# Second feed-forward: relu and square of the block chunk two pieces later, and its transposes apart from the ordinary chunk's

## The chip, the core and the metric

One core of one Trainium2 chip runs the whole program. The metric is the device time of one execution in microseconds (us), the median of three runs; one further execution was profiled, and all rows below come from it. TensorE (PE in the rows, PEld for its weight loads) multiplies, VectorE (DVE) and ScalarE (ACT) work elementwise and read PE's results out of the PSUM banks, SyncE (SP) issues the loads of weights.

## The reference

Two transformer blocks on 256 tokens of 2048 features. Only the end of the second one is touched, its feed-forward part:

```python
h2 = rms_norm(x, g_ff[l])
x = x + jnp.square(jax.nn.relu(h2 @ w_ff1[l])) @ w_ff2[l]      # w_ff1: 2048 x 8192, w_ff2: 8192 x 2048
```

All data are float32. The kernel splits each operand into a high part (rounded to PE's format) and a low part (the rest), and adds three products for each product of the reference: high by high, high by low, low by high.

## The kernel before

**Pieces.** A weight matrix is streamed in pieces of 512 KB. For each piece SP loads it into a raw buffer (R, or G for a block piece), ACT rounds it to its high part in W (L230), DVE subtracts to get the low part (L232), and PE multiplies. All engines work their instructions off in the order in which the program was written. That order is written out by a list of jobs: before a piece is multiplied, the splits (L230, L232) of the pieces up to three further on are written, as far as their slots in W have been given up by earlier pieces.

**The second feed-forward** has four groups (`gi`). A group makes 2048 of the 8192 columns of `h2 @ w_ff1` and at once multiplies them into the output. It has two *braids* and then four *down chunks*.

- A braid makes 1024 columns. It weaves an *ordinary chunk* of 8 pieces (called a0 to a7 here; L262 to L264, 12 matmuls of 512 columns each, PSUM banks 4 and 5) with a *block chunk* of 8 pieces (b0 to b7; L315 to L317, 21 matmuls of 256 columns each, Strassen's scheme with seven products for eight, banks 0 to 3). The order is a0 a1 b0 a2 b1 a3 b2 a4 b3 a5 b4 a6 b5 a7, the ordinary chunk's end, b6 b7, the block chunk's end. For a block piece DVE also makes sums of weights ahead of its split (L207 to L209).
- The ordinary chunk's end is relu and square by ACT, from PSUM into `abuf` (in G). The block chunk's end, `fin`, has one copy by ACT (L328), four additions by DVE that put the seven products together into G and `tmp` (L329 to L332), and then relu and square by ACT in place: four instructions (L1191 and L1192, twice).
- PE then needs the 1024 columns with tokens along the free axis: 16 transposes for each chunk pair, 8 of `abuf` and 8 of the block chunk's `half` (L387). Four of them fill one of the two PSUM banks 6 and 7; out of each bank ACT writes the high part into B (L374) and DVE the low part (L375). These 16 transposes with their four L374 and four L375 are one job, `pending`: the first braid's stands in the second braid, behind a2 (fourth piece) and ahead of b1; the second braid's stands in the first down chunk, behind its fourth piece.
- A down chunk has 8 pieces (called p0 to p7) of `w_ff2`, ordinary ones, multiplied with the transposed columns in B.

**The first feed-forward** has braids of the same order; there the block chunk's end is done by DVE, and only one chunk's 8 transposes are `pending`.

Of the kernel before, what the change touches and what calls it, by code (L numbers as in the profile page):

```python
# [19 lines left out]
KT = D // P  # L20
# [5 lines left out]
QW = 256  # L26
PLAIN, MIX, STR = 0, 1, 2
# [44 lines left out]
def body(tc, d, out):  # L72
# [4 lines left out]
    with tc.manual_schedule(), \  # L77
# [7 lines left out]
        G = res.tile([P, 8192], F32, name="G")  # L85
# [5 lines left out]
        tmp = res.tile([P, 512], F32, name="tmp")  # L91
# [4 lines left out]
        def rview(t, off, *dims):  # L96
            n = int(np.prod(dims))
            v = t[:, off : off + n]
            if len(dims) == 2:
                return v.rearrange("p (a b) -> p a b", a=dims[0])  # L100
            if len(dims) == 3:
                return v.rearrange("p (a b c) -> p a b c", a=dims[0], b=dims[1])
            if len(dims) == 4:
                return v.rearrange("p (a b c e) -> p a b c e", a=dims[0], b=dims[1], c=dims[2])
            return v
# [26 lines left out]
        def bank_at(b):  # L132
            return PS[:, b * 512 : (b + 1) * 512]
# [7 lines left out]
        jobs = []  # L141
        before_dma, before_split = {}, {}

        def run(fn):
            jobs.append(("run", fn))

        def stage(m):
            run(lambda: mode.__setitem__(0, m))
# [103 lines left out]
        def piece(src, fn, lo=True, post=None, kind=PLAIN):  # L252
            return ("pc", src, fn, lo, post, kind)
# [7 lines left out]
        def mm3(o, x, w, first, last):  # L261
            pe.matmul(o, x[0], w[0], start=first, stop=False)  # L262
            pe.matmul(o, x[0], w[1], start=False, stop=False)  # L263
            pe.matmul(o, x[1], w[0], start=False, stop=last)  # L264

        def chunk(pair, w, kts, c0, n, evict, row0=0, inject=None, kind=PLAIN, fixed=None):

            items, banks = [], list(fixed or ())

            def mk(j):  # L270
                def fn(h, l):
                    if j == 0 and not fixed:
                        banks.extend([FREE.pop(0) for _ in range(NT)])
                    for q in range(2):
                        kt = 2 * j + q
                        for tok in range(NT):
                            mm3(bank_at(banks[tok])[:, :n], pair(kt, tok), (h[:, q, :], l[:, q, :]), kt == 0, kt == kts - 1)
                return fn

            for j in range(kts // 2):  # L280
                if inject and j in inject:
                    items.append(("run", inject[j]))
                items.append(piece(wsrc(w, row0 + 2 * j, c0, n), mk(j), kind=kind))

            def fin():
                for tok in range(NT):
                    evict(tok, bank_at(banks[tok])[:, :n])
                if not fixed:
                    FREE.extend(banks)

            items.append(("run", fin))
            return items

        def strassen(pair, forms, w, kts, c0, evict):

            items = []

            prod = [(("x", 0, 0), 0, 2, 1), (("x", 1, 0), 1, 0, 0), (("s", 3), 2, 3, 0), (("x", 1, 1), 6, 2, 0),  # L300
                    (("s", 0), 3, 1, 1), (("s", 1), 5, 0, 1), (("s", 2), 4, 1, 0)]

            def mk(j):
                def fn(h, l):
                    opened = set()
                    for x, wi, bank, half in prod:
                        o = PS[:, bank * 512 + half * QW : bank * 512 + (half + 1) * QW]
                        if x[0] == "x":
                            xh, xl = pair(2 * j + x[1], x[2])
                        else:  # L310
                            xh, xl = forms[:, 0, j, x[1], :], forms[:, 1, j, x[1], :]
                        first = j == 0 and bank not in opened
                        opened.add(bank)
                        last = j == kts // 2 - 1
                        pe.matmul(o, xh, h[:, wi, :], start=first, stop=False, skip_group_check=True)  # L315
                        pe.matmul(o, xl, h[:, wi, :], start=False, stop=False, skip_group_check=True)  # L316
                        pe.matmul(o, xh, l[:, wi, :], start=False, stop=last, skip_group_check=True)  # L317
                return fn

            for j in range(kts // 2):  # L320
                items.append(piece(wsrc(w, 2 * j, c0, 512), mk(j), kind=STR))

            def fin():
                q = PS[:, 0:2048].rearrange("p (a b) -> p a b", a=8)
                u = rview(G, 1024, 4, QW)
                v = tmp.rearrange("p (a b) -> p a b", a=2)
                bc = [P, 2, QW]
                act.copy(v[:, 0, :], q[:, 5, :])  # L328
                dve.tensor_tensor(u[:, 0:2, :], v[:, 0:1, :].to_broadcast(bc), q[:, 0:2, :], op=ALU.add)  # L329
                dve.tensor_tensor(u[:, 2:4, :], u[:, 1:2, :].to_broadcast(bc), q[:, 2:4, :], op=ALU.add)  # L330
                dve.tensor_tensor(v[:, ::-1, :], u[:, 2:3, :].to_broadcast(bc), q[:, 3:5, :], op=ALU.add)
                dve.tensor_tensor(u[:, 3, :], u[:, 3, :], q[:, 6, :], op=ALU.add)  # L332
                evict(0, u[:, 0:4:3, :])
                evict(1, v)

            items.append(("run", fin))
            return items

        def braid(a, b, inject=None):

            pa, pb = [x for x in a if x[0] == "pc"], [x for x in b if x[0] == "pc"]
            order = [pa[0], pa[1]]
            for i in range(6):
                order += [pb[i], pa[i + 2]]
            order += [a[-1], pb[6], pb[7], b[-1]]
            for at in sorted(inject or {}, reverse=True):
                order.insert(at, ("run", inject[at]))
            return order
# [182 lines left out]
        def blocks(nat):  # L531
            return lambda tok, i: nat[:, tok, i * P : (i + 1) * P]
# [259 lines left out]
        for p in range(9):  # L792
            a, b, c = plan[p]
# [54 lines left out]
        pending = wide(oT_late, "w_attn_o", ev_mix, t_mix, None, kts=8, row0=8)  # L848
# [33 lines left out]
        h2T = pairat(A, 0, KT)  # L882
        h2F = rview(C, 0, 2, KT // 2, 4, P)
        pending = wide(mixT, "w_out", ev_res(tmp, inv2), t_x(h2T, "ffn", h2F), pending, last=MIX)


        abuf = rview(G, 0, NT, 512)
# [9 lines left out]
        def t_a(aT, nat, j):  # L897
            return lambda: transposed(nat, aT, list(range(4 * j, 4 * j + 4)))
# [11 lines left out]
        for gi, (c0, nch) in enumerate(groups):  # L910
            aT = pairat(B, 0, 16)
            for j in range(nch):
                c = c0 + j
# [3 lines left out]
                pending = t_a(aT, blocks(abuf), j)  # L917
            lastg = gi == len(groups) - 1
            for oc in range(4):
                inj = {}  # L920
                if pending is not None:
                    inj[nch * 2 - 4 if oc == 0 else 1] = pending
                    pending = None
                ev = ev_res(tmp, inv3)(oc) if lastg else ev_acc(oc)
                jobs.extend(chunk(aT, "w_ffn_down", 4 * nch, oc * 512, 512, ev, row0=4 * c0, inject=inj,
                                  kind=MIX, fixed=DOWN[oc]))
                if lastg:
                    pending = t_x(hT, "mix")(oc)
# [250 lines left out]
        pending = None  # L1179
        for c in range(4):  # L1180
# [3 lines left out]
            pending = t_mer(c)  # L1184

        inv4 = stat(2)
        pending = wide(merT, "w_out_2", ev_res(tmp, inv4), t_x(h2T, "ff", h2F), pending, last=MIX)


        def relu2(o, tok, v):  # L1190
            act.activation(o, v, AF.Relu, scale=inv4[:, tok : tok + 1])  # L1191
            act.activation(o, o, AF.Square)  # L1192
# [3 lines left out]
            v = rview(G, 1024, 4, QW)[:, 0:4:3, :] if tok == 0 else tmp.rearrange("p (a b) -> p a b", a=2)  # L1196
            return v[:, i // 2, (i % 2) * P : (i % 2 + 1) * P]

        def two(f, g):
            return lambda: (f(), g())  # L1200

        def ev_out(c):
            def f(tok, ps):
                xs = xnat[:, tok, c * 512 : (c + 1) * 512]
# [2 lines left out]
            return f  # L1207

        stage(MIX)
        for gi in range(4):  # L1210
            aT = pairat(B, 0, 16)
            for j in range(0, 4, 2):
                c = 4 * gi + j
                jobs.extend(braid(chunk(h2T, "w_ff1_2", KT, c * 512, 512,
                                        lambda tok, ps: relu2(abuf[:, tok, :], tok, ps), kind=MIX, fixed=(4, 5)),
                                  strassen(h2T, h2F, "w_ff1_2", KT, (c + 1) * 512, lambda tok, v: relu2(v, tok, v)),
                                  {4: pending} if pending is not None else None))
                pending = two(t_a(aT, blocks(abuf), j), t_a(aT, half, j + 1))
            for oc in range(4):
                inj = {}  # L1220
                if pending is not None:
                    inj[4] = pending
                    pending = None
                ev = ev_out(oc) if gi == 3 else ev_acc(oc)
                jobs.extend(chunk(aT, "w_ff2_2", 16, oc * 512, 512, ev, row0=16 * gi, inject=inj,
                                  kind=MIX, fixed=DOWN[oc]))

        drive()

# [80 lines left out]
```

## Time and profile before

| | us |
|---|---|
| median of 3 runs | 2766.05 (2765.75 to 2766.68) |
| the profiled execution, its own time | 2765.54 |
| its span, first to last instruction | 2763.8 |
| PE busy in the span | 2722.0 |
| DVE busy | 1854.9 |
| ACT busy | 1404.2 |

The span is what the trace covers; 1.74 us of the execution's own time lie outside it. Busy times overlap between engines. The second feed-forward runs from about 2018 us to the end of the span.

### The profile page before, as it was taken

The numbers are of one execution on the slowest core, as the hardware profiler recorded it, in microseconds if no ns is written. First come the engines' busy times: TensorE is split into PE (matmuls) and PEld (weight loads), VectorE is DVE, ScalarE is ACT, GpSimd is POOL, SyncE is SP. The second block draws the span as 40 slices with busy tenths as digits, with TensorE's granted clock in tenths as the row PEclk, the third lists the DMA queues.
The fourth block names the chain that finished last, engine by engine and source line by source line (L and its number), as shares of the span: only waits on it lengthen the run. The fifth ranks groups of instructions, "written<-read, shape, count | busy, mean of one in ns | idle before, by whom it ended". The sixth has DMA issues, their size and how long they took to land. (4 is left out here: it accounts for less than half of the span.)

```text
span 2763.8 us, 35989 instructions
## 1 busy us (share of the span) xinstructions
PE 2722.0 (98%) x13996; PEld 2285.7 (83%) x13996; DVE 1854.9 (67%) x2233; ACT 1404.2 (51%) x1749; POOL 72.8 (3%) x153
## 2 busy tenths in 40 slices
PE   9999999999999999999999999999989999999999
PEld 8988888888888888888888888888778878877877
DVE  6554677767995799489655565555686685775774
ACT  6544666545554455355555554443554454453553
POOL 1000111000000000000010100000000000000000
PEclk9999999999999999999999999999999999999999
DMA  7666444554555655555464555555554645645545
GB/s 256 210 209 199 160 138 142 179 177 173 206 191 176 213 183 191 185 204 198 156 212 164 199 177 171 191 187 183 174 177 152 202 173 166 210 142 188 201 153 167
DMA packets 143179, 506.66 MB, mean 183 GB/s; under 512 B 16160, under 2 KB 18592, under 8 KB 142496
## 3 DMA queue, kind: packets, MB, share of 16 engines
q1 hardware_dynamic: 142864, 504.31, 54.2%
q8 instruction: 109, 1.79, 0.3%
q14 instruction: 62, 0.51, 0.1%
q10 hardware_dynamic: 144, 0.05, 0.0%
HBM read 502.21 MB, written 2.10 MB: 182 GB/s over the span
## 5 line engine op out<-in xcount | busy, mean ns | idle before, releaser
L232 DVE TENSOR_TENSOR W<-R,W 128x1024 fp32r<-128x1024 f32 (+2 forms) x795 | 943.2, 1208 | 527.6 <-ACT W L230 525.0
L230 ACT CAST W<-R 128x1024 fp32r<-128x1024 f32 (+2 forms) x798 | 810.0, 1035 | 533.2 <-PE PS L264 439.6
L262 PE MATMUL PS<-W,A 128*128 128x512 f32 (+2 forms) x1728 | 678.6, 393 | 5.6 <-ACT W L230 5.4
L263 PE MATMUL PS<-W,A 128*128 128x512 f32 (+2 forms) x1728 | 678.8, 393 | 5.2 <-DVE W L232 5.2
L264 PE MATMUL PS<-W,A 128*128 128x512 f32 (+2 forms) x1728 | 676.4, 391 | 0.0
L262 PE MATMUL PS<-W,B 128*128 128x512 f32 (+1 forms) x1248 | 491.7, 394 | 0.0
L263 PE MATMUL PS<-W,B 128*128 128x512 f32 (+1 forms) x1248 | 489.5, 392 | 0.9 <-DVE W L232 0.9
L264 PE MATMUL PS<-W,B 128*128 128x512 f32 (+1 forms) x1248 | 489.3, 392 | 0.0
L230 ACT CAST W<-G 128x1792 fp32r<-128x1792 f32 x152 | 257.3, 1693 | 316.3 <-PE PS L316 155.3
L263 PEld LDWEIGHTS PS<-W,A 128*128 128x128 f32 x1728 | 324.7, 188 | 75.5 <-DVE W L232 9.2
L262 PEld LDWEIGHTS PS<-W,A 128*128 128x128 f32 x1728 | 324.5, 188 | 74.1 <-ACT W L230 6.3
L264 PEld LDWEIGHTS PS<-W,A 128*128 128x128 f32 x1728 | 324.3, 188 | 73.6
L232 DVE TENSOR_TENSOR W<-G,W 128x1792 fp32r<-128x1792 f32 x152 | 307.1, 2020 | 53.4 <-ACT W L230 53.4
L263 PEld LDWEIGHTS PS<-W,B 128*128 128x128 f32 x1248 | 234.1, 188 | 55.1 <-DVE W L232 2.1
L264 PEld LDWEIGHTS PS<-W,B 128*128 128x128 f32 x1248 | 233.9, 187 | 54.1
L262 PEld LDWEIGHTS PS<-W,B 128*128 128x128 f32 x1248 | 234.0, 188 | 53.9
L315 PE MATMUL PS<-W,C 128*128 128x256 f32 x608 | 170.2, 280 | 0.0
L317 PE MATMUL PS<-W,C 128*128 128x256 f32 x608 | 169.8, 279 | 0.0
L316 PE MATMUL PS<-W,C 128*128 128x256 f32 x608 | 169.6, 279 | 0.0
L315 PE MATMUL PS<-W,A 128*128 128x256 f32 x456 | 130.6, 286 | 0.0
L317 PE MATMUL PS<-W,A 128*128 128x256 f32 x456 | 128.4, 282 | 0.8 <-DVE W L232 0.8
L316 PE MATMUL PS<-W,A 128*128 128x256 f32 x456 | 128.4, 282 | 0.0
(231 smaller groups left out, 2496.5 us busy)
## 6 DMA issues: line engine op xcount, KB each, us to landing
R<-in_w_in_dram SPq DMA_DIRECT2D x224, 512.0 KB, 4.6
R<-in_w_ff_dram SPq DMA_DIRECT2D x192, 512.0 KB, 3.6
R<-in_w_ffn_gate_dram SPq DMA_DIRECT2D x88, 512.0 KB, 4.4
G<-in_w_ffn_up_dram SPq DMA_DIRECT2D x88, 512.0 KB, 3.5
R<-in_w_ffn_down_dram SPq DMA_DIRECT2D x88, 512.0 KB, 3.5
R<-in_w_out_dram SPq DMA_DIRECT2D x64, 512.0 KB, 4.4
G<-in_w_ff_dram SPq DMA_DIRECT2D x64, 512.0 KB, 3.5
R<-in_w_attn_o_dram SPq DMA_DIRECT2D x32, 512.0 KB, 4.4
```

The costliest lines, as they stand in the source:

```text
L230: act.copy(hv, v)
L232: dve.tensor_tensor(lv, v, hv.bitcast(F32), op=ALU.subtract)
L262: pe.matmul(o, x[0], w[0], start=first, stop=False)
L263: pe.matmul(o, x[0], w[1], start=False, stop=False)
L264: pe.matmul(o, x[1], w[0], start=False, stop=last)
L315: pe.matmul(o, xh, h[:, wi, :], start=first, stop=False, skip_group_check=True)
L316: pe.matmul(o, xl, h[:, wi, :], start=False, stop=False, skip_group_check=True)
L317: pe.matmul(o, xh, l[:, wi, :], start=False, stop=last, skip_group_check=True)
```

## The change

The block chunk's relu and square (`ends`) no longer stand at the end of `fin` in the second feed-forward; they become a job of their own. The pending job is cut into three. In the next braid: the 8 transposes of `abuf` behind a0 (T1), `ends` behind a1, the 8 transposes of `half` behind b2 (T2). In the first down chunk: `ends` behind p0, T1 behind p1, T2 behind p3. No instruction is added or dropped, and no load changes its place.

```diff
-        def strassen(pair, forms, w, kts, c0, evict):
+        def strassen(pair, forms, w, kts, c0, evict, later=False):
...
                 dve.tensor_tensor(u[:, 3, :], u[:, 3, :], q[:, 6, :], op=ALU.add)
-                evict(0, u[:, 0:4:3, :])
-                evict(1, v)
+                if not later:
+                    ends()
+
+            def ends():
+                evict(0, rview(G, 1024, 4, QW)[:, 0:4:3, :])
+                evict(1, tmp.rearrange("p (a b) -> p a b", a=2))
 
             items.append(("run", fin))
-            return items
+            return (items, ends) if later else items
...
         stage(MIX)
+        pending = {4: pending}
...
-                jobs.extend(braid(chunk(h2T, "w_ff1_2", KT, c * 512, 512,
-                                        lambda tok, ps: relu2(abuf[:, tok, :], tok, ps), kind=MIX, fixed=(4, 5)),
-                                  strassen(h2T, h2F, "w_ff1_2", KT, (c + 1) * 512, lambda tok, v: relu2(v, tok, v)),
-                                  {4: pending} if pending is not None else None))
-                pending = two(t_a(aT, blocks(abuf), j), t_a(aT, half, j + 1))
+                plain = chunk(h2T, "w_ff1_2", KT, c * 512, 512, lambda tok, ps: relu2(abuf[:, tok, :], tok, ps),
+                              kind=MIX, fixed=(4, 5))
+                block, ends = strassen(h2T, h2F, "w_ff1_2", KT, (c + 1) * 512, lambda tok, v: relu2(v, tok, v), later=True)
+                jobs.extend(braid(plain, block, pending))
+                pending = {1: t_a(aT, blocks(abuf), j), 2: ends, 7: t_a(aT, half, j + 1)}
             for oc in range(4):
-                inj = {}
-                if pending is not None:
-                    inj[4] = pending
+                inj = None
+                if oc == 0:
+                    inj = {1: pending[2], 2: pending[1], 4: pending[7]}
                     pending = None
```

Numbers ahead of a job say in front of which entry of the list it is put. The order on PE, ACT and DVE changes from this; on SP and POOL it stays. From line 334 on, the changed kernel's lines are numbered some four higher: L1195 and L1196 there are L1191 and L1192 here, L378 and L379 are L374 and L375.

ACT where the first braid of a group passes into the second, before. L328 is `fin`'s copy; the casts after the four activations are those of a2, b1, a3, b2:

```order
L328 COPY tmp<-PS 128x256
L1191 ACTIVATE G<-G,st 128x2x256
L1192 ACTIVATE G<-G 128x2x256
L1191 ACTIVATE tmp<-tmp,st 128x512
L1192 ACTIVATE tmp<-tmp 128x512
L230 CAST W<-R 128x1024
L230 CAST W<-G 128x1792
L230 CAST W<-R 128x1024
L230 CAST W<-G 128x1792
L374 CAST B<-PS 128x512 x4
```

The same place on ACT after the change:

```order
L328 COPY tmp<-PS 128x256
L230 CAST W<-R 128x1024
L378 CAST B<-PS 128x512 x2
L230 CAST W<-G 128x1792
L1195 ACTIVATE G<-G,st 128x2x256
L1196 ACTIVATE G<-G 128x2x256
L1195 ACTIVATE tmp<-tmp,st 128x512
L1196 ACTIVATE tmp<-tmp 128x512
L230 CAST W<-R 128x1024
L230 CAST W<-G 128x1792
L230 CAST W<-R 128x1024
L230 CAST W<-G 128x1792
```

The cast of a2, two of the four casts of transposed columns and the cast of b1 now stand ahead of the four activations; the other two L378 follow one cast further down, behind that of a5.

DVE at the same place, before: `fin`'s four additions, the low part of a2, then the sums of b2 and the low part of b1 (the L375 follow ten rows further down):

```order
L329 TENSOR_TENSOR G<-tmp,PS 128x512
L330 TENSOR_TENSOR G<-G,PS 128x512
L331 TENSOR_TENSOR tmp<-G,PS 128x2x256
L332 TENSOR_TENSOR G<-G,PS 128x256
L232 TENSOR_TENSOR W<-R,W 128x1024
L207 TENSOR_TENSOR G<-G 128x512
L208 TENSOR_TENSOR G<-G 128x256
L209 TENSOR_TENSOR G<-G 128x256
L232 TENSOR_TENSOR W<-G,W 128x1792
```

DVE at the same place after the change:

```order
L332 TENSOR_TENSOR G<-G,PS 128x256
L232 TENSOR_TENSOR W<-R,W 128x1024
L379 TENSOR_TENSOR B<-PS,B 128x512 x2
L207 TENSOR_TENSOR G<-G 128x512
L208 TENSOR_TENSOR G<-G 128x256
L209 TENSOR_TENSOR G<-G 128x256
L232 TENSOR_TENSOR W<-G,W 128x1792
```

Two of the four subtractions of transposed columns came forward, between the low part of a2 and that of b1; the other two stand behind the low part of a5.

ACT where the second braid passes into the first down chunk, after the change. The casts are those of p3, then p4 and p5, then p6 and on:

```order
L328 COPY tmp<-PS 128x256
L1195 ACTIVATE G<-G,st 128x2x256
L1196 ACTIVATE G<-G 128x2x256
L1195 ACTIVATE tmp<-tmp,st 128x512
L1196 ACTIVATE tmp<-tmp 128x512
L230 CAST W<-R 128x1024
L378 CAST B<-PS 128x512 x2
L230 CAST W<-R 128x1024 x2
L378 CAST B<-PS 128x512 x2
```

Here the activations keep their place; before, the casts of p3, p4 and p5 stood together, and all four L374 behind them.

## Rows read from the trace of the kernel before

**Rows 1.** The page: its first line, and PE in part 1.

```profile
span 2763.8 us, 35989 instructions
...
PE 2722.0 (98%) x13996; PEld 2285.7 (83%) x13996; DVE 1854.9 (67%) x2233; ACT 1404.2 (51%) x1749; POOL 72.8 (3%) x153
```

**Rows 2.** Waits of PE, 2025 to 2764: total us, times, longest.

```profile
PE PS L387 <- DVE B L375: 23.7, 8, 5.0
PE PS L262 <- ACT W L230: 4.7, 4, 1.2
PE PS L263 <- DVE W L232: 3.8, 5, 0.8
```

**Rows 3.** Timeline of PE, first group, second braid: start, us, [idle before, releaser].

```profile
2049.59 0.40 PE L262 MATMUL PS<-W,A 128*128 128x512 f32 x1
...
2055.28 0.36 PE L315 MATMUL PS<-W,A 128*128 128x256 f32 x1
...
2057.69 0.28 PE L317 MATMUL PS<-W,C 128*128 128x256 f32 x1
2059.15 0.51 PE L262 MATMUL PS<-W,A 128*128 128x512 f32 x1 [1.18 <-ACT W L230]
2060.41 0.50 PE L263 MATMUL PS<-W,A 128*128 128x512 f32 x1 [0.76 <-DVE W L232]
2060.75 0.39 PE L264 MATMUL PS<-W,A 128*128 128x512 f32 x1
...
2063.07 1.03 PE L387 MATMUL PS<-cst,G 128*128 128x128 f32 x8
2069.06 0.41 PE L387 MATMUL PS<-cst,G 128*128 128x128 f32 x1 [4.96 <-DVE B L375]
...
2070.62 0.56 PE L315 MATMUL PS<-W,A 128*128 128x256 f32 x1
...
2072.66 0.28 PE L315 MATMUL PS<-W,A 128*128 128x256 f32 x1
```

**Rows 4.** Timeline of ACT there.

```profile
2055.50 0.72 ACT L1191 ACTIVATE G<-G,st 128x512 f32<-128x512 f32 x1 [5.55 <-DVE G L332]
...
2058.07 1.03 ACT L230 CAST W<-R 128x1024 fp32r<-128x1024 f32 x1
...
2063.71 1.07 ACT L374 CAST B<-PS 128x512 fp32r<-128x512 f32 x2
```

**Rows 5.** Timeline of DVE there.

```profile
2052.94 0.68 DVE L329 TENSOR_TENSOR G<-tmp,PS 128x512 f32<-128x512 f32 x1
...
2055.05 0.41 DVE L332 TENSOR_TENSOR G<-G,PS 128x256 f32<-128x256 f32 x1
2059.13 1.23 DVE L232 TENSOR_TENSOR W<-R,W 128x1024 fp32r<-128x1024 f32 x1 [3.67 <-ACT W L230]
...
2061.80 2.02 DVE L232 TENSOR_TENSOR W<-G,W 128x1792 fp32r<-128x1792 f32 x1
...
2068.32 1.28 DVE L375 TENSOR_TENSOR B<-PS,B 128x512 fp32r<-128x512 f32 x2
```

**Rows 6.** Stretches: from:to, us, busy of PE, PEld, DVE, ACT, POOL, PEclk, DMA.

```profile
2070.00:2071.00 1.00, 1.00 (x7) 1.00 (x6) 0.23 (x1) 0.59 (x1) 0.00 (x0) 0.50 0.86 344
```

**Rows 7.** Timeline of PE, first group, first down chunk, behind its fourth piece.

```profile
2113.94 1.03 PE L387 MATMUL PS<-cst,G 128*128 128x128 f32 x8
2115.94 0.33 PE L387 MATMUL PS<-cst,G 128*128 128x128 f32 x1 [0.96 <-DVE B L375]
...
2117.27 0.39 PE L263 MATMUL PS<-W,B 128*128 128x512 f32 x1
```

**Rows 8.** Timeline of PE in a braid of the first feed-forward.

```profile
981.33 1.03 PE L387 MATMUL PS<-cst,G 128*128 128x128 f32 x8
982.12 0.37 PE L315 MATMUL PS<-W,A 128*128 128x256 f32 x1
982.32 0.28 PE L316 MATMUL PS<-W,A 128*128 128x256 f32 x1
```

**Rows 9.** Timeline of PE, fourth group, second braid.

```profile
2632.64 0.47 PE L387 MATMUL PS<-cst,G 128*128 128x128 f32 x1 [4.95 <-DVE B L375]
```

More of the change, by code (lines that the diff above doesn't have):

```diff
@@ L1197, in half @@
             return v[:, i // 2, (i % 2) * P : (i % 2 + 1) * P]
-        def two(f, g):
-            return lambda: (f(), g())
         def ev_out(c):
```

## Prediction

> **What bounds the kernel now.** I read the page first. PE is busy for 2722.0 of 2763.8 us [rows 1], so it is the engine that sets the end, and only time in which PE stands still or runs slowly can be won. The second view is PE's waits in the stretch that the change touches. Nearly all of them have three causes: transposes that wait for VectorE's subtraction out of PSUM (23.7 us in 8 waits), and a piece that waits for its cast (4.7) and its low part (3.8) [rows 2]. Eight waits are two for each of the four groups, so the third view is the timeline of one group, PE first, then the engines that it waits for.
>
> PE there [rows 3]: the second braid begins at 2049.59 with a0 and a1, b0 follows at 2055.28, and its last matmul starts at 2057.69. Then a2 waits 1.18 us for its cast and 0.76 us for its low part. Behind a2 the first 8 transposes start at 2063.07, and the next 8 wait 4.96 us, until 2069.06, because the two banks are still full.
>
> Why a2 is late stands on ACT [rows 4]: behind the copy ACT sits idle for 5.55 us, waiting for the last of VectorE's additions, then runs four activations, and the cast of a2, which needed none of that, starts only at 2058.07. DVE in turn has done its last addition at 2055.05 + 0.41 = 2055.46 and then sits idle for 3.67 us until that cast [rows 5]. It comes out of this late, has the low parts and sums of further pieces in front of it, and reaches the subtractions of the transposed columns only at 2068.32 [rows 5], although ACT had cast both banks from 2063.71 on [rows 4]. That is PE's wait of 4.96 us.
>
> When PE starts again, it runs at half pace for a while: the granted clock is 0.50 in 2070 to 2071 [rows 6], the lower of its two levels (1.2 GHz for 2.4). The matmuls of b1 between 2070.62 and 2072.66 are nine steps in 2.04 us [rows 3], 0.23 each against 0.12 at full clock (20 steps from 2055.28 to 2057.69). Before the fall PE had stood still for those 4.96 us.
>
> The second place is the first down chunk, where the second 8 transposes wait 0.96 us [rows 7]. The fourth group shows the same wait as the first, 4.95 us, and lies 563.58 us later, three times 187.86 [rows 9, 3]: the groups are alike, and what holds for one is taken four times.
>
> **The change, part by part.** No instruction is added, and none changes its size. So the sum is what PE loses at each place today, less what it will lose there. I take losses from start to start, since ends of matmuls overlap the next.
>
> Full pace comes from these rows: a 512-column matmul 0.232 us (2060.75 to 2063.07 are ten steps [rows 3]), so an ordinary piece 12 x 0.232 = 2.78 us; a 256-column one 0.12, a block piece 2.5; 8 transposes without a wait 0.79 us (981.33 to 982.12), after which the next step takes 0.20 for 0.12, so 0.87 in all [rows 8].
>
> *a2's wait.* From 2057.69 to 2060.75 PE made three steps in 3.06 us; at full pace 0.12 + 2 x 0.23 = 0.58. Loss 2.48.
>
> *The transposes and the slow clock.* From 2063.07 to 2070.62 are 16 transposes, 7.55 us for 2 x 0.79 = 1.58: loss 5.97. The nine steps to 2072.66 took 2.04 for 0.20 + 8 x 0.12 = 1.16: loss 0.88. Two separate runs of transposes pay the longer step twice, 0.08 back. Together 6.77.
>
> *The down chunk.* From 2113.94 to 2117.27 are 3.33 us [rows 7]; two runs of 0.87 and one step of 0.23 are 1.97. Loss 1.36.
>
> That makes 10.6 us a group, 42.4 us in four. Whether all of it goes is a question of what replaces the waits, and I walk the new order by hand, with the durations above.
>
> PE: a0 at 2049.59, T1 at 2052.37, a1 at 2053.24, b0 at 2056.0, a2 at 2058.5, b1 at 2061.3, a3 at 2063.8, b2 at 2066.6, T2 at 2069.1, a4 at 2070.0, b3 at 2072.7. ACT: the cast of a2 follows the copy at once, some 2050, and is done at 2051; the first bank of T1 is full 0.64 us after its start (2063.07 to 2063.71 [rows 3, 4]), so two L374 run from 2053.0 to 2054.1; the cast of b1 ends at 2055.8. Now the four activations run, 2.57 us (2055.50 to 2058.07), and nothing that they wait for is late: the additions end at 2055.46. They are done at 2058.4, T2 needs them at 2069.1.
>
> DVE is the engine to watch. After the last addition it goes on at once with the low part of a2 (2055.46 to 2056.6, needed at 2058.5), two L375 (1.28 for two [rows 5], to 2057.85), the sums of b2 and the low part of b1. Before, low part of a2, sums and the start of b1's low part were 2061.80 - 2059.13 = 2.67 apart, 1.53 of it sums; so b1's low part runs from 2059.4 to 2061.4. PE starts b1 at 2061.3 and needs the low part at its third matmul, 2061.5. That is even, with 0.1 to 0.2 us to spare; I charge 0.1 a group. Behind it DVE needs 1.14 + 1.53 + 1.94 = 4.6 us for a pair of pieces, PE 5.3, so the lead grows: a3 is ready at 2062.5, b2 at 2066.0, a4 at 2067.1, b3 at 2070.6, each ahead of PE. The bounds of the charge are nothing and the 1.28 us of the two L375, which are new in front of b1.
>
> The transposes' banks: T2 needs them 11 us after T1's were read out, so this wait goes. With no wait above 0.3 us left on PE there, the clock has no standstill to fall after. In the down chunk PE reaches p3 some 9 us after p0, and DVE there has one low part of 1.23 us per 2.78 us of PE; T1 behind p1 and T2 behind p3 lie two pieces apart, 5.6 us, against about 3 us for casts and subtractions of two banks. Loss there nothing. SP's queue keeps its order, and the loads of b3 and b4 hang on the low parts of b0 and b1 (2053.0 and 2061.4 against sums due some 9 and 5 us later).
>
> Sum: 4 x (10.6 - 0.1) = 42.0 us. The profiled execution took 2765.54 us on its own (span 2763.8 and 1.74 around it), which leaves 2723.5; the median shown lies 0.5 above that execution, so **2724.0 us**, 1.5% less.
>
> A second way to count gives less: the idle times listed, 4 x (1.18 + 0.76 + 4.96 + 0.96) = 31.4 us. The Trainium skill (Perfetto Trace Analysis, Identifying the Most-Contended Engine) says that matmul busy time is no good measure, since pipelined matmuls hide it, and to look at weight loads. This trace agrees: PE 98% busy, its weight loads 83% [rows 1]. By busy time the sum would be 31.4 us, by starts it is 42.4.
>
> **The rivals.**
>
> *A new wait at b1.* DVE's chain in front of b1 has almost no slack. If one step of it comes the 1.28 us of two L375 later, PE waits 1.1 us a group: 2728. For it: the walk's margin. Against: DVE stays without idle time from 2052.94 on.
>
> *Only the listed idle time comes back*, because a shorter new wait still lets the clock fall or the slow steps have another cause: 2766.05 - 31.4 = 2734.6. Against it: clock 0.50 stands right behind the long wait.
>
> *It doesn't do what it says:* the transposes wait for the same two banks as ever, now in two places, 2766. It needs L375 of T1 to slip behind T2, by 11 us.
>
> *Slower.* T2 makes ACT and DVE wait for PE in the middle of a braid: its L374 and L375 stand in front of the split of b4. From T2's start they need 0.64 + 1.07 + 0.65, then sums 1.53 and low part 2.02, 5.9 us; PE reaches b4 after 0.87 + 2.78 + 2.5 + 2.78 = 8.9. Spare 3.0. Only when that chain comes 3 us later does PE wait, and it must wait 10.6 us a group to undo the gain, 12 to end at 2772. The Trainium skill (PSUM — Partial Sum Buffer, Engine vs sequencer instructions) calls the queues of ScalarE and VectorE strictly first in, first out; the trace agrees, where the cast of a2 stood behind activations that waited [rows 4]. It is this rule by which each moved cast can hold up what follows, and which speaks against a second stop.
>
> **How the numbers follow.** Forecast as worked out 0.73; new wait at b1 0.13; only the idle time 0.07; no effect 0.03; slower 0.04. 0.2%, 5.5 us, is about what a measurement of this kernel can tell from no change; so faster 0.93, same 0.03, slower 0.04. The range reaches from 2719 (all of 42.4 won, and some small extra steps of the same places) to 2735, the case of idle time alone.
>
> **What would show it.** In the profile after: PE's waits on L379 gone, or below 1 us in all; no stretch of the second feed-forward with granted clock 0.50; groups 177 us apart instead of 187.86; ACT's cast of a2 directly behind the copy; DVE without the idle 3.67 us behind its additions; the four activations with no wait. Wrong it would be if PE waited at b1 for L232 by more than 0.5 us, or at b4, or at p4 for B, or if the clock still fell in each group.

## The result, and the profile after

The changed kernel takes 2722.7 us (median of 4 runs, 2722.05 to 2723.18) against 2765.9 before (median of 4 runs): ratio 0.9843, 95% interval 0.9829 to 0.9856, so 1.4 to 1.7% faster. The forecast was 2724.0, range 2719 to 2735. The profiled execution took 2722.61, 42.9 less than that of before; the sum had said 42.0.

The page's first line and the engines' busy times, after, which answer to [rows 1]:

```profile
span 2720.9 us, 35965 instructions
...
PE 2709.6 (100%) x13996; PEld 2278.4 (84%) x13996; DVE 1851.8 (68%) x2233; ACT 1402.6 (52%) x1749; POOL 73.0 (3%) x153
```

PE's waits from 2025 us on, which answer to [rows 2]:

```profile
PE PS L263 <- DVE W L232: 0.9, 1, 0.9
PE PS L317 <- DVE W L232: 0.4, 1, 0.4
```

One long stretch (us, busy of PE, PEld, DVE, ACT, POOL, granted clock, DMA share, GB/s), which answers to [rows 6]:

```profile
2047.00:2720.00 673.00, 669.11 (x3536) 567.17 (x3535) 467.00 (x502) 334.77 (x340) 0.00 (x0) 1.00 0.55 186
```

DVE and ACT are busy as long as before, within some 3 us. The first line counts 24 instructions fewer, but none of the five engine rows below it has another count, so they are among those that the page does not count as busy. PE has lost 31 us of waits, and the two that remain lie at 2025.66 and 2029.12, in the first braid, where the change has nothing. From 2047 on no wait is left and the clock is at its upper level throughout. PE's busy time fell too, by 12.4 us, though it has the same matmuls. About 6 us of that are the slow clock (e7 below), under which a matmul counts as busy for longer; the rest are by the rows mainly the matmuls around a wait, which count in full where others overlap: b0's last one is listed with 0.28 us [rows 3], and where no wait follows the next starts 0.11 us later (2058.46 and 2058.57 below). That is the part that a count of idle time does not see.

The passage from the first braid of a group into the second, timeline of PE; L391 is L387 of before (T1 at the top, T2 at the bottom):

```profile
2052.44 1.04 PE L391 MATMUL PS<-cst,G 128*128 128x128 f32 x8
2053.24 0.48 PE L262 MATMUL PS<-W,A 128*128 128x512 f32 x1
...
2058.46 0.28 PE L317 MATMUL PS<-W,C 128*128 128x256 f32 x1
2058.57 0.39 PE L262 MATMUL PS<-W,A 128*128 128x512 f32 x1
2058.80 0.40 PE L263 MATMUL PS<-W,A 128*128 128x512 f32 x1
...
2061.60 0.28 PE L317 MATMUL PS<-W,A 128*128 128x256 f32 x1
...
2069.07 0.27 PE L391 MATMUL PS<-cst,G 128*128 128x128 f32 x1
```

Timeline of ACT there; L378 is L374 of before, L1195 is L1191:

```profile
2049.63 0.36 ACT L328 COPY tmp<-PS 128x256 f32<-128x256 f32 x1
2049.89 1.05 ACT L230 CAST W<-R 128x1024 fp32r<-128x1024 f32 x1
2053.08 1.07 ACT L378 CAST B<-PS 128x512 fp32r<-128x512 f32 x2 [2.14 <-PE PS L391]
2054.04 1.71 ACT L230 CAST W<-G 128x1792 fp32r<-128x1792 f32 x1
2055.63 0.73 ACT L1195 ACTIVATE G<-G,st 128x512 f32<-128x512 f32 x1
```

Timeline of DVE there; L379 is L375 of before:

```profile
2055.09 0.41 DVE L332 TENSOR_TENSOR G<-G,PS 128x256 f32<-128x256 f32 x1
2055.42 1.22 DVE L232 TENSOR_TENSOR W<-R,W 128x1024 fp32r<-128x1024 f32 x1
2056.55 1.28 DVE L379 TENSOR_TENSOR B<-PS,B 128x512 fp32r<-128x512 f32 x2
...
2059.27 2.02 DVE L232 TENSOR_TENSOR W<-G,W 128x1792 fp32r<-128x1792 f32 x1
```

Against [rows 3, 4, 5]: the cast of a2 follows the copy at 2049.89 instead of 2058.07; the activations start without a wait; DVE goes from its last addition into a2's low part without the idle 3.67 us; and a2's first two matmuls are 0.23 us apart where they were 1.26. The low part of b1 is ready at 2059.27 + 2.02 = 2061.29, and its first reader, b1's third matmul, starts at 2061.60: 0.3 us to spare. T2 starts at 2069.07, walked by hand at 2069.1.

T2 of the next group starts at 2246.14 (same kind of row), 177.07 us later; groups were 187.86 apart, and 177 were forecast.

### The profile page after: what moved, and what is told of

It reads as the page before. It is cut to its first block, busy times and chain, and to the rows that moved or that the text cites. A ratio compares the mean times of both kernels' runs of the same rounds, so it can differ in the third digit from the quotient of the medians.

```text
span 2720.9 us, 35965 instructions
## 1 busy us (share of the span) xinstructions
PE 2709.6 (100%) x13996; PEld 2278.4 (84%) x13996; DVE 1851.8 (68%) x2233; ACT 1402.6 (52%) x1749; POOL 73.0 (3%) x153
```

## The experiments

All eight change the second feed-forward alone. Times are medians; each was run in turn with the kernel before, whose median is given where it is compared.

**e1: only the activations later.** The 16 transposes stay one job.

```diff
-                pending = {1: t_a(aT, blocks(abuf), j), 2: ends, 7: t_a(aT, half, j + 1)}
+                pending = {2: ends, 4: two(t_a(aT, blocks(abuf), j), t_a(aT, half, j + 1))}
...
-                    inj = {1: pending[2], 2: pending[1], 4: pending[7]}
+                    inj = {1: pending[2], 4: pending[4]}
```

> One part alone: the four activations of the block chunk's end move two pieces later (one in the down chunk), all 16 transposes stay one job at the old place, behind a2 and behind p3. Theory (the bank wait is DVE reaching the subtractions late, out of two causes: its idle time behind the additions, and the splits in front): a2's wait of 2.48 us goes, DVE starts 3.67 us earlier, the second 8 transposes still wait, some 3.7 us instead of 4.96. Walked by hand: 3.95 us a group lost in the braid and 1.3 in the down chunk against the changed kernel's 2722.7, so 2744, up to 2750 if the clock still falls after the shorter wait. Rival (the wait is that of two banks alone and doesn't depend on when DVE is free): it stays at 5 us with the slow clock, only a2's 2.48 us come back, 2756.

Measured 2751.0 (2749.95 to 2751.41; ratio to before 0.9945, 0.9933 to 0.9958). Timeline of PE, its two waits in the first group:

```profile
2064.98 0.47 PE L391 MATMUL PS<-cst,G 128*128 128x128 f32 x1 [3.65 <-DVE B L379]
...
2111.82 0.33 PE L391 MATMUL PS<-cst,G 128*128 128x128 f32 x1 [0.96 <-DVE B L379]
```

A stretch right behind the longer one, and then DVE's first subtractions in its timeline:

```profile
2066.00:2067.00 1.00, 1.00 (x7) 1.00 (x6) 0.26 (x1) 0.60 (x2) 0.00 (x0) 0.50 1.00 377
```

```profile
2064.24 1.28 DVE L379 TENSOR_TENSOR B<-PS,B 128x512 fp32r<-128x512 f32 x2
```

The wait on the banks is 3.65 us, 3.7 were expected. a2's wait is gone, and DVE without idle time reaches the subtractions at 2064.24 instead of 2068.32 [rows 5]; so the bank wait depends on when DVE is free, which the rival denied. The clock still falls behind 3.65 us of standstill, in all four groups, which brings the time 1.0 us above the upper end of the expectation.

**e2: only the transposes apart.** The activations stay in `fin`.

```diff
-                pending = {1: t_a(aT, blocks(abuf), j), 2: ends, 7: t_a(aT, half, j + 1)}
+                pending = {1: t_a(aT, blocks(abuf), j), 7: t_a(aT, half, j + 1)}
...
-                    inj = {1: pending[2], 2: pending[1], 4: pending[7]}
+                    inj = {2: pending[1], 4: pending[7]}
```

> The other part alone: the transposes are taken apart (T1 behind a0, T2 behind b2; behind p1 and p3 in the down chunk), the four activations stay at the block chunk's end, ahead of the cast of a2. Theory: no wait on banks and no slow clock, but the cast of a2 still starts at about 2058.1, DVE is idle 3.7 us, and with T1's two subtractions in front of b1 its low part comes at about 2065: PE waits 1.6 us at a2 and about 1.75 at b1, 13.4 us in four groups, 2736. Rival (the activations' place does not matter once the transposes are apart): 2723. Second rival (only a2's old wait of 2.48 us stays, nothing new at b1): 2732.6.

Measured 2737.1 (2736.73 to 2737.76; ratio 0.9896, 0.9883 to 0.991). Timeline of PE, its waits in the first group, then DVE's of the same passage, and a long stretch:

```profile
2059.74 0.49 PE L262 MATMUL PS<-W,A 128*128 128x512 f32 x1 [0.47 <-ACT W L230]
2061.00 0.50 PE L263 MATMUL PS<-W,A 128*128 128x512 f32 x1 [0.76 <-DVE W L232]
2065.65 0.39 PE L317 MATMUL PS<-W,A 128*128 128x256 f32 x1 [1.58 <-DVE W L232]
```

```profile
2059.72 1.23 DVE L232 TENSOR_TENSOR W<-R,W 128x1024 fp32r<-128x1024 f32 x1 [3.67 <-ACT W L230]
```

```profile
2047.00:2700.00 653.00, 641.66 (x3408) 544.01 (x3407) 454.26 (x490) 325.70 (x332) 0.00 (x0) 1.00 0.55 186
```

DVE's idle 3.67 us are back to the hundredth, and PE pays them at a2 and, new, at b1. No wait on banks is left and the granted clock is 1.00. Both rivals fall. So each half of the change takes away what the other leaves: alone they are worth 15.1 (e1) and 29.0 us (e2) against the kernel before's 2766.05 of those runs, together 43.2, about their sum of 44.0.

**e3: T1's subtractions done twice** in each second braid, otherwise the changed kernel (`transposed` repeats its last line there).

```diff
+                    if twice:
+                        dve.tensor_tensor(pair.v[:, 1, ks[0] : ks[-1] + 1, :], s,
+                                          pair.v[:, 0, ks[0] : ks[-1] + 1, :].bitcast(F32), op=ALU.subtract)
...
-                pending = {1: t_a(aT, blocks(abuf), j), 2: ends, 7: t_a(aT, half, j + 1)}
+                pending = {1: t_a(aT, blocks(abuf), j, twice=j == 0), 2: ends, 7: t_a(aT, half, j + 1)}
```

> The changed kernel with T1's two subtractions on DVE done twice in each second braid (same data written again), 1.2 to 1.3 us more DVE work in front of b1's low part. Theory (DVE's chain in front of b1 has 0.2 to 0.3 us to spare): PE waits about 1.0 us a group at b1, 2726.7. Rival (the chain has room, b1 is not the tight place): 2722.7.

Measured 2727.7 (2727.18 to 2727.92). The wait in the first group, in the timeline of PE:

```profile
2062.72 0.39 PE L317 MATMUL PS<-W,A 128*128 128x256 f32 x1 [1.05 <-DVE W L232]
```

It is b1's third matmul, 1.02 to 1.05 us in each group, 4.2 of the 5.0 us that were lost, 1.25 a group. The repeated subtractions let b1's low part start at 2060.65 instead of 2059.27, 1.4 us later. The spare time in front of b1 is as small as the walk said.

**e8: the same doubled subtractions, T1 behind a2.**

```diff
-                pending = {1: t_a(aT, blocks(abuf), j, twice=j == 0), 2: ends, 7: t_a(aT, half, j + 1)}
+                pending = {4: t_a(aT, blocks(abuf), j, twice=j == 0), 2: ends, 7: t_a(aT, half, j + 1)}
```

> The kernel with T1's subtractions done twice (e3: 2727.7), but T1 behind a2 instead of behind a0, so that its subtractions stand behind b1's and b2's low parts on DVE instead of in front. Theory (the added subtractions cost time in e3 only because they stood in front of b1): DVE's lead takes them, 2722.7. Rival (DVE has no room for them anywhere in the braid): 2727.7.

Measured 2723.1 (2722.84 to 2723.67). PE's waits are the two of the first braid again. The same work costs nothing that stands out behind b2's low part, and 1.25 us a group in front of b1's. It is the place that counts, not DVE's load in the braid.

**e4: T2 behind a2**, where the whole job stood before; T1 and the activations as in the change.

```diff
-                pending = {1: t_a(aT, blocks(abuf), j), 2: ends, 7: t_a(aT, half, j + 1)}
+                pending = {1: t_a(aT, blocks(abuf), j), 2: ends, 4: t_a(aT, half, j + 1)}
```

> The changed kernel with T2 three pieces earlier, behind a2, where the whole job stood before; T1 and the activations as in the changed kernel. Theory (what matters is that T1's banks are read out before T2 starts, here by 2058 against some 2061): no bank wait, 2722.7. Rival (the distance between T1 and T2, or T2's late place, is what brings the gain): a bank wait of some us a group comes back, 2735 or more.

Measured 2722.2 (2721.69 to 2722.63), the same as the change within the spread of either, and with no wait on banks in its profile. So T2 needs no late place; it needs T1's banks read out.

**e5: the change in the down chunks alone.**

```diff
-                block, ends = strassen(h2T, h2F, "w_ff1_2", KT, (c + 1) * 512, lambda tok, v: relu2(v, tok, v), later=True)
+                block = strassen(h2T, h2F, "w_ff1_2", KT, (c + 1) * 512, lambda tok, v: relu2(v, tok, v), later=j == 2)
+                if j == 2:
+                    block, ends = block
...
+                both = t_a(aT, blocks(abuf), j), t_a(aT, half, j + 1)
+                pending = {4: two(*both)}
...
+                    inj = {1: ends, 2: both[0], 4: both[1]}
```

> The change in the down chunks alone (activations behind p0, T1 behind p1, T2 behind p3); where the first braid passes into the second all stays as before. Theory: 1.36 us a group come back, 5.4 in four, 2760.5, the braid's waits and slow clock as before. Rival (the down chunk's wait is made up for elsewhere): 2766.

Measured 2758.3 against 2765.6 (ratio 0.9975, 0.9966 to 0.9985), with runs spread from 2756.1 to 2762.4. The four waits in the down chunks are gone. The second 8 transposes of the first two groups start at 2068.35 and 2254.81, 186.46 us apart instead of 187.84: 1.38 us, 1.36 expected. The spread goes with the clock: in the second, third and fourth group of the profiled run (2761.8 us) it is down already between a2 and the transposes, which in the profile of the kernel before happened in no group. Timeline of PE in the third group, the stretch between, and one further on:

```profile
2432.73 0.50 PE L263 MATMUL PS<-W,A 128*128 128x512 f32 x1 [0.77 <-DVE W L232]
...
2441.37 0.47 PE L391 MATMUL PS<-cst,G 128*128 128x128 f32 x1 [3.40 <-DVE B L379]
```

```profile
2434.00:2435.00 1.00, 1.00 (x4) 0.80 (x3) 1.00 (x2) 0.73 (x1) 0.00 (x0) 0.50 0.00 0
...
2446.00:2447.00 1.00, 1.00 (x7) 1.00 (x7) 0.97 (x3) 0.00 (x0) 0.00 (x0) 0.50 0.00 0
```

The slow steps behind a2 cost little by themselves: PE reaches the full banks later and waits 3.40 us for them instead of 4.95 in the first group. The cost lies behind the transposes, where in the third and fourth group the clock stays down about twice as long as in the first two. From the third group's second transposes (2441.37) to the fourth's (2628.94) are 187.57 us, against 186.56 from the second's to the third's: 1.0 us of the 1.38 is gone again.

Runs with a mean clock of 0.996 took 2756.1 to 2759.4, those with 0.993 and 0.994 2761.8 to 2762.4. Why the former lie more than 5.4 us below the kernel before was not profiled and stays open.

**e6: the kernel before with added matmuls in the long wait.**

```diff
+        def busy():
+            for _ in range(40):
+                pe.matmul(PS[:, 3 * 512 + QW : 4 * 512], h2T(0, 0)[0], h2T.v[:, 0, 1, :], start=False, stop=False,
+                          skip_group_check=True)
...
-                pending = two(t_a(aT, blocks(abuf), j), t_a(aT, half, j + 1))
+                pending = two(t_a(aT, blocks(abuf), j), two(busy if j == 0 else lambda: None, t_a(aT, half, j + 1)))
```

> The kernel before with 40 added matmuls of 256 columns between the first and the second 8 transposes in each second braid; their result goes to a half bank that nobody reads. They keep PE at work for about 4.7 of the 4.96 us of its wait. Theory (the clock falls because PE stands still, and the slow stretch costs 0.77 us in the transposes and 0.88 behind them): granted clock 1.00 throughout, 6.6 us less than before, 2759.3. Rival (the steps are slow for another cause, or the slow clock costs nothing on the path): 2766 or more.

Measured 2762.5 against 2765.6 (ratio 0.9989, 0.998 to 0.9998): 3.1 us less, not the theory's 6.6. In the first two groups it went as expected: in the first the added matmuls fill 2063.21 to the second transposes at 2068.39, and the clock stays up. In the third and fourth the clock fell before them, behind a2's wait. Timeline of PE, one stretch of the first and the third group each, and the second transposes in the first down chunk of each group:

```profile
2063.21 5.04 PE L1204 MATMUL PS<-A 128*128 128x256 f32 x40
```

```profile
2069.00:2070.00 1.00, 1.00 (x10) 1.00 (x10) 0.30 (x1) 0.91 (x2) 0.00 (x0) 1.00 0.58 164
...
2434.00:2435.00 1.00, 1.00 (x3) 0.74 (x3) 1.00 (x2) 0.92 (x1) 0.00 (x0) 0.50 0.00 0
```

```profile
2113.83 0.33 PE L387 MATMUL PS<-cst,G 128*128 128x128 f32 x1 [0.96 <-DVE B L375]
...
2300.23 0.33 PE L387 MATMUL PS<-cst,G 128*128 128x128 f32 x1 [0.96 <-DVE B L375]
...
2487.78 0.33 PE L387 MATMUL PS<-cst,G 128*128 128x128 f32 x1 [0.97 <-DVE B L375]
...
2675.21 0.33 PE L387 MATMUL PS<-cst,G 128*128 128x128 f32 x1 [0.97 <-DVE B L375]
```

So the experiment did not do what it was meant to: it left a second standstill in, a2's. As a whole it leaves the size open, but the groups tell it. From one of these four starts to the next are 186.40, 187.55 and 187.43 us; in the kernel before, where the first of them lies at 2115.94 [rows 7], they were 187.81, 187.93 and 187.70. In the second group, where the clock stayed up, 1.4 us came back, in the third and fourth 0.4 and 0.3.

**e7: e1 with added matmuls**, where a2 has no wait (28 of them, the same lines as in e6).

> The kernel of the ends alone (e1: 2751.0, with a wait of 3.65 us and the granted clock at 0.50 behind it in each group) with 28 added matmuls of 256 columns between the first and the second 8 transposes in each second braid, into a half bank that nobody reads; there is no wait at a2 in it that could bring the clock down by itself. Theory (the slow steps come from PE's standstill, and cost 1.5 to 1.65 us a group): clock 1.00 in all groups, 6.0 to 6.6 us less than e1, 2744.5. Rival (they don't count on the path): 2751.

Measured 2744.5 (2744.21 to 2745.09), 6.5 us less than e1, with work added. Each against the kernel before of its own runs, e7 gains 21.1 us and e1 15.1, a difference of 6.0. The stretch behind the transposes, and the whole stage:

```profile
2066.00:2067.00 1.00, 1.00 (x11) 1.00 (x10) 1.00 (x2) 1.00 (x2) 0.00 (x0) 1.00 0.91 344
...
2047.00:2700.00 653.00, 647.92 (x3482) 549.54 (x3481) 451.34 (x486) 324.51 (x328) 0.00 (x0) 1.00 0.54 183
```

The clock is 1.00 and PE starts 11 matmuls in that microsecond where e1 started 7. The slow clock is thus a cost of its own, 1.5 to 1.6 us a group, and comes from PE standing still: fill the standstill with work that nobody needs, and it goes.

## Why the prediction was right, step by step

*a2's wait, 2.48 us a group.* It came from a cast queued behind activations that waited on DVE. After the change the row is gone; e2, with the activations back, brings DVE's idle 3.67 us back exactly. Part of it returns there as PE's wait (0.47 and 0.76), for PE comes 0.87 us later through T1.

*The bank wait, 5.97 us with the slow steps in the transposes.* The walk said that it has two causes, DVE late and splits in front. e1 takes the first away and leaves 3.65 of 4.96; the change, e2 and e4 take the transposes apart, and it is gone in all three, in e2 although DVE is as late as before.

*The slow clock, 0.77 in the transposes (a part of the 5.97) and 0.88 behind them.* e7 shows it to be worth 6.0 to 6.5 us in four groups, and e6 1.4 in the one group that can be told apart, against 4 x 1.65 = 6.6: counted right, or a little high.

*The down chunk, 1.36 us.* e5: 1.38 by the distance of the first two groups.

*The charge at b1, 0.1 us.* PE did not wait there in any group. With 0.3 us to spare this was mis-sized, a little, to the safe side. e3 and e8 show that the chain in front of b1 was rightly called tight: 1.4 us more there cost 1.25.

The sum was 0.9 us too small, and 0.4 of that is this charge. Most of the rest lies where the walk saw no loss, at the start of b0 in each second braid. Before, PE's steps there began at 2054.96, 2055.28 and 2055.47, 0.32 and 0.19 us apart; after, at 2055.89, 2056.12 and 2056.24, 0.23 and 0.12. That is 0.16 us a group, 0.6 in four. The long steps are there in e1 and e8 too, where T1 does not stand behind a0, and not in e2, e3 and e4, where it does; why, no run shows. Against it, the first braid waited 0.92 us at its first low part, where before it was 0.71 (2025.59).

*The two ways of counting.* By listed idle time 31.4 us were to come back, by starts 42.4; 43 came. What separates them is the slow clock and the overlapping ends of matmuls; the rival that rested on idle time alone fell.

*The rivals.* No new wait appeared at b1, so the first fell, though e3 shows how near it was. The third, two banks as ever, fell with the waits. The slower one named T2 as a second stop in ACT and DVE: ACT does stand there, 3.04 us until 2069.71, and still nothing follows from it. Its price was off, without harm: the chain left out a5's low part, which DVE does ahead of T2's subtractions. So b4's low part was done 7.2 us behind T2's start and not 5.9 (2074.24 + 2.02 against 2069.07), and as PE reached b4 at 2077.99, some 1.7 us were spare and not 3.0. e4 takes T2 out of this place altogether and is no faster.

## What to carry to other kernels

Where an engine works strictly in order, look at what stands *behind* an instruction that waits: the activations here were in no hurry, and the cast behind them was. When a job needs more buffers than there are, split it and put other work between the halves, for as long as the engine that empties the buffers needs. And before adding work to the emptying engine, walk its chain up to the next thing that the bound engine reads: the same two subtractions, done again, cost nothing that stands out in one place and 1.25 us a group, almost all of their time, in another.

## What was not expected of the hardware

The clock fell not only behind PE's waits of 5 and 3.65 us: in e5 and e6 it fell in some groups (2 to 4 in e5, 3 and 4 in e6) and not in others behind a2's, listed as 1.18 and 0.76 us, with the same waits in front of it. In e6 the first group ran at 1.00 behind a2 and the third at 0.50. In the profile of the kernel before it fell behind none of the four. A wait of that size may or may not bring its slow stretch, and what the stretch costs depends on what stands behind it: in e5 most of it fell into a wait that was there anyway, in e6 the added matmuls took that wait's place, and the groups with it won 1.0 us less. A sum over one profile can't tell.
